# Small parameters of the heads and sinks in one array, and one cache load further back in the load queue

## The chip, the cores and the metric

The kernel runs on one core of one Trainium2 chip. The metric is the device time of one execution in microseconds (us). Before the change it is 1283.69 us, the median of three runs (1283.01 to 1283.9).

TensorE (PE) multiplies, VectorE (DVE), ScalarE (ACT) and GpSimd (POOL) do the elementwise work, and SyncE (SP) issues almost every transfer between HBM and on-chip memory.

## The reference, cut to what matters

One step of an encoder with four layers (A, B, C, A) over 512 prompt tokens and 64 sample tokens of width 1024, all in fp32. Each layer computes

```python
z = rmsnorm(x, norm_g) @ w_in                 # q, k, v and a gate
q = rmsnorm(q_per_head, q_g); k = rmsnorm(k_per_head, k_g)
o = attend(q, k, v, scale, bias, mask, sinks) # sinks in layer B alone
x = x + (o * silu(gate)) @ w_out
```

The small parameters are `q_g` and `k_g` of each layer (128 numbers in A, 64 in B, 96 in C) and B's 16 `sinks`, which enter the softmax of each head as one more score. B also reads a cache of 128 older keys per key head (`cache_bkT`).

## The kernel before, in words

**Precision.** A product is formed from high and low halves: a tile `ws` of weights is split into `wh` (ACT, line 121) and `wl` = `ws` - `wh` (line 122; on POOL in the first microseconds, later on DVE), and the same is done with the transposed activations `T` (ACT line 182 for the high half, DVE line 183 for the low one). Three matmuls (lines 164, 165, 166) then make one product.

**Start.** The five token tiles of `x` (four of 128 rows, one of 64) are loaded, normalised and transposed in `norm`. Each tile takes two halves of 512 columns: DVE scales a half (line 194, output `qs`, or `half` for the tile of 64 rows), PE transposes it with four instructions (`t`, line 179), ACT and DVE write the high and low half of `T`. Between the transposes PE already runs the first matmuls of layer A on the tiles that are there. The weights for these come in four transfers (line 129); the next weights, eight tiles `ws` of two transfers each, come after `flip` and `flip2` (line 132). There are four buffers `ws`, two PSUM buffers `t`, three buffers `qs`. A buffer `ws` is free for the next load when its `wl` has been computed.

**Order.** A scheduler decides at build time the order of the instructions on each engine; each engine then runs its own list in that order and waits where an input is missing. A transfer on SP's list also waits for the one eight places before it on that list (they share one of eight completion counters). That is the program's own rule. It has one effect on reading the profile: a wait for a transfer can be put down to a later transfer on the same counter. The instruction `nsks` (line 467) waits in the program for the two `sks` loads, and the profile names `cqg` for it.

**Small parameters.** Layers A, B and C load them where they are first written in the source (lines 276 and 110, 456 to 465, 688), and the scheduler put most of these loads, and B's cache load (line 482), among the first weight loads of layer A. The sinks per pair of heads are read with a stride:

```python
ld(sks[64 * e : 64 * e + 64], I["b_sinks"].rearrange("o (j e) -> o j e", e=2)[:, :, e].to_broadcast([64, 8]))
```

A few DVE instructions scale or negate them (lines 277, 458, 462, 467, 689), in the order that the scheduler gave them among DVE's other work.

**End of a layer.** `load_x` reads `x` again (line 105), `gain` the next norm's weights (line 936), and `out_proj` loads `w_out` in two halves of eight tiles (line 132), multiplies and adds; `norm` then makes the next `T`.

Of the kernel before, what the change touches and what calls it, by code (L numbers as in the profile page):

```python
# [9 lines left out]
F32 = mybir.dt.float32  # L10
# [4 lines left out]
ALU = mybir.AluOpType  # L15
# [4 lines left out]
KD = 8  # L20
SEQ = 512
DEC = 64
TOK = SEQ + DEC
# [8 lines left out]
CT = (7,)  # L32
# [4 lines left out]
WT = 2 * TOK + DEC  # L37
# [3 lines left out]
def encoder_step(ctx: ExitStack, tc: tile.TileContext, I, O):  # L41
    nc = tc.nc
    V, S, G, PE = nc.vector, nc.scalar, nc.gpsimd, nc.tensor
    ld = nc.sync.dma_start

    const = ctx.enter_context(tc.tile_pool(name="const", bufs=1))
# [7 lines left out]
    def sb(n, tag, bufs=None, dt=F32, pool=work):  # L54
        return pool.tile([128, n], dt, tag=tag, name=tag, bufs=bufs)
# [23 lines left out]
    flip = sb(128, "flip", pool=const)  # L79
    flip2 = sb(128, "flip2", pool=const)  # L80

    mhalf = sb(1, "mhalf", pool=const)
    V.memset(mhalf, -0.5)

# [11 lines left out]
        return half[turn[0]]  # L96

    x = []
    weng = [V]

    def load_x(pool, src):
        x.clear()
        for t, (t0, tn) in enumerate(TT):
            xt = sb(D, f"x{t}", pool=pool)
            ld(xt[:tn], src[t0 : t0 + tn, :])
            x.append(xt)

    def col(src, n, tag, parts=128):
        c = sb(n, tag, pool=const)
        ld(c[:parts], src)  # L110
        return c

    def rstd(ss, tn, n, inv):
        r = sb(n, "nv", pool=tiny)[:tn]
# [70 lines left out]
    def norm(t, g, xT):  # L185
        t0, tn = TT[t]
        ss = sb(1, "nss", pool=tiny)[:tn]
        junk = sb(D, "sq", 2, dt=BF16)[:tn]
        S.activation(junk, x[t][:tn], AF.Square, accum_out=ss)
        r = rstd(ss, tn, 1, 1.0 / D)  # L190
        for hf in range(2):
            xs = rows_of(tn)
            cs = slice(hf * 512, hf * 512 + 512)
            V.scalar_tensor_tensor(out=xs[:tn], in0=x[t][:tn, cs], scalar=r, in1=g[:tn, cs], op0=ALU.mult, op1=ALU.mult)
            pt = v3(ps_t(), 128)
            for j in range(4):
                tr(pt[:, j, :], xs[:, j * 128 : j * 128 + 128])
            k0 = hf * 4
            l0 = lo_at(t0, TOK)
            hl_evac(xT[:, k0 : k0 + 4, t0 : t0 + tn], xT[:, k0 : k0 + 4, l0 : l0 + tn], pt[:, :, :tn])  # L200
            if tn == DEC:
                V.tensor_copy(xT[:, k0 : k0 + 4, 2 * TOK : WT], xT[:, k0 : k0 + 4, TOK : TOK + DEC].bitcast(F32))

    def og_tiles():
        pairs = [v3(sb(2 * TOK, f"o{b}", pool=ogp), TOK) for b in range(KD // 2)]
# [36 lines left out]
    def mix(main, fill):  # L242
        n, f = len(main), 0
        for i, u in enumerate(main):
            u()
            while f < len(fill) * (i + 1) // n:
                fill[f]()
                f += 1
# [23 lines left out]
    def layer_a(li, xT, first=None):  # L272
        w = I["a_w_in"][li]
        with tc.tile_pool(name=f"la{li}", bufs=1, reuse_waits="tile") as lp:
            qg = sb(1, f"qg{li}", pool=const)
            ld(qg, I["a_q_norm"][li].rearrange("(p o) -> p o", o=1))
            V.tensor_scalar(out=qg, in0=qg, scalar1=128 ** -0.5, scalar2=None, op0=ALU.mult)
            kg = col(I["a_k_norm"][li].rearrange("(p o) -> p o", o=1), 1, f"kg{li}")
            ogs, _ = og_tiles()
            vs, qks = {}, {}  # L280

# [167 lines left out]
    def layer_b(xT):  # L449
        w = I["b_w_in"][0]  # L450
        with tc.tile_pool(name="lb", bufs=1, reuse_waits="tile") as lp:
            qg = sb(1, "bqg", pool=const)
            kg = sb(1, "bkg", pool=const)
            for e in range(2):
                r = slice(64 * e, 64 * e + 64)
                ld(qg[r], I["b_q_norm"][0].rearrange("(p o) -> p o", o=1))
                ld(kg[r], I["b_k_norm"][0].rearrange("(p o) -> p o", o=1))
            V.tensor_scalar(out=qg, in0=qg, scalar1=64 ** -0.5, scalar2=None, op0=ALU.mult)
            sk = sb(16, "sk", pool=const)
            ld(sk, I["b_sinks"].to_broadcast([128, 16]))  # L460
            nsk = sb(16, "nsk", pool=const)
            V.tensor_scalar(out=nsk, in0=sk, scalar1=-1.0, scalar2=None, op0=ALU.mult)
            sks = sb(8, "sks", pool=const)
            for e in range(2):
                ld(sks[64 * e : 64 * e + 64], I["b_sinks"].rearrange("o (j e) -> o j e", e=2)[:, :, e].to_broadcast([64, 8]))
            nsks = sb(8, "nsks", pool=const)
            V.tensor_scalar(out=nsks, in0=sks, scalar1=-1.0, scalar2=None, op0=ALU.mult)
            ogs, pairs = og_tiles()

            def rsb(n, tag, bufs=1):  # L470
# [7 lines left out]
            ld(vc, I["cache_b_v"][0, 0].rearrange("t h d -> t (h d)"))  # L478

            kst = v3(sb(512, "hl", 1), 128)  # L480
            for e in range(2):
                ld(kst[64 * e : 64 * e + 64], I["cache_bkT"].rearrange("h p t -> p h t"))
            split(kch[:, :, :128], kcl[:, :, :128], kst)

            def hl(h, l, src, g):
# [4 lines left out]
            for t, (t0, tn) in enumerate(TT):  # L490
                p = mm_tok(xT, TOK, t0, tn, pieces, 512)
# [5 lines left out]
                r = rstd(ss, tn, 4, 1.0 / 64)  # L497
# [177 lines left out]
    def layer_c(xT):  # L675
        w = I["c_w_in"][0]
        with tc.tile_pool(name="lc", bufs=1, reuse_waits="tile") as lp:
            scale = 96 ** -0.5
            early = [sb(512, "ex", 4) for _ in range(3)]
            qag = early[2]  # L680
            ld(qag, I["c_q_a_norm"].to_broadcast([128, 512]))
            kvg = early[0][:, :256]
            ld(kvg, I["c_kv_a_norm"].to_broadcast([128, 256]))
            qgc = sb(1, "cqg", pool=const)
            kgc = sb(1, "ckg", pool=const)
            for g, nm in ((qgc, "c_q_norm"), (kgc, "c_k_norm")):
                V.memset(g[:96], 1.0)
                ld(g[:64], I[nm][0, :64].rearrange("(p o) -> p o", o=1))
            V.scalar_tensor_tensor(out=qgc[:96], in0=qgc[:96], scalar=scale, in1=kgc[:96], op0=ALU.mult, op1=ALU.mult)
            cs = v3(sb(512, "sq", 2)[:, :160], 32)  # L690
            sn_ = v3(sb(512, "sq", 2)[:, :160], 32)
            for tab, nm in ((cs, "rope_cos"), (sn_, "rope_sin")):
# [3 lines left out]
            for nm in ("c_q_norm", "c_k_norm"):  # L696
# [8 lines left out]
                for (sl, rows) in ((slice(0, 4), 128), (slice(4, 5), 64)):  # L705
                    n = sl.stop - sl.start
                    V.tensor_tensor(out=ta[:rows, sl], in0=cs[:rows, sl], in1=bc(gb[:rows].unsqueeze(1), rows, n, 32), op=ALU.mult)
                    for a, b in ((0, 16), (16, 0)):
                        V.tensor_tensor(out=tb[:rows, sl, a : a + 16], in0=sn_[:rows, sl, a : a + 16],
                                        in1=bc(gb[:rows, b : b + 16].unsqueeze(1), rows, n, 16), op=ALU.mult)  # L710
# [25 lines left out]
            for t, (t0, tn) in enumerate(TT):  # L736
                p = mm_tok(xT, TOK, t0, tn, pieces, 512)
# [3 lines left out]
                r = rstd(ss, tn, 1, 1.0 / 512)  # L741
                c = rows_of(tn)
# [8 lines left out]
            for t, (t0, tn) in enumerate(TT):  # L751
                p = mm_tok(xT, TOK, t0, tn, pieces, 288)
# [4 lines left out]
                r = rstd(ss, tn, 2, [(0, 1, 1.0 / 256), (1, 2, 1.0 / 32)])  # L757
                cf = rows_of(tn)[:, :256]
                c = cf[:tn]
# [13 lines left out]
                k0 = 128 * kt  # L773
# [166 lines left out]
    xT = big_xT()  # L940
    first = []
    weng[0] = G
    with tc.tile_pool(name="xp0", bufs=1) as xp:
        for t, (t0, tn) in enumerate(TT):
            xt = sb(D, f"x{t}", pool=xp)
            ld(xt[:tn], I["x"][t0 : t0 + tn, :])
            x.append(xt)
            if t == 0:
                ld(ident, I["ident"])
                nxt_gain = gain(xp, "a", 0)  # L950
            if t < 4:
                src = I["a_w_in"][0][256 * t : 256 * t + 256, 2048:2304].rearrange("(a p) c -> p a c", p=128)
                h, l = load_w([src], 512, 256)
                first += [(h[:, 256 * i : 256 * i + 256], l[:, 256 * i : 256 * i + 256]) for i in range(2)]
            norm(t, nxt_gain, xT)
        ld(flip, I["flip"])
        ld(flip2, I["flip2"])
    dp = ctx.enter_context(tc.tile_pool(name="dp", bufs=1, space=bass.MemoryType.DRAM))
    x_src = I["x"]
    for i, (kind, li) in enumerate(layers):  # L960
        if kind == "a":
            ogs, tail = layer_a(li, xT, first if i == 0 else None)
        elif kind == "b":
            ogs, tail = layer_b(xT)
        else:
            ogs, tail = layer_c(xT)
        x_new = dp.tile([TOK, D], F32, tag=f"xd{i}", name=f"xd{i}") if i < 3 else O["y"]
        nxt = {}

        def after(t, nh):  # L970
            t0, tn = TT[t]
            if i == 3:
                ld(x_new[t0 : t0 + tn, nh * 512 : nh * 512 + 512], x[t][:tn, nh * 512 : nh * 512 + 512])
            elif nh == 1:
                if "xT" not in nxt:
                    nxt["xT"] = big_xT()
                ld(x_new[t0 : t0 + tn], x[t][:tn])
                norm(t, nxt_gain, nxt["xT"])

        with tc.tile_pool(name=f"op{i}", bufs=1, reuse_waits="tile") as op:  # L980
            oT = v3(sb(KD * WT, "oT", dt=F32R, pool=op), WT)

            def put(b):
                split_o(oT, b, ogs[b])

            units = tail(put)
            late = {"a": (6, 7), "b": (6, 7), "c": CT}[kind]
            mix([lambda b=b: put(b) for b in range(KD) if b not in late], units)
            load_x(op, x_src)
            if i < 3:  # L990
                nxt_gain = gain(op, *layers[i + 1])
            out_proj(I[f"{kind}_w_out"][li], oT, after)
        x_src = x_new
        xT = nxt.get("xT")
# [91 lines left out]
```

## Time and profile before

| | |
|---|---|
| median of three runs | 1283.69 us |
| the profiled execution | 1283.49 us |
| its span | 1281.7 us |
| PE busy in the span | 1244.6 us (97%) |
| DVE, ACT, POOL busy | 715.8, 647.7, 383.6 us |
| PE, DVE and ACT in the chain that ended last | 91%, 4%, 2% |

The span runs from the first to the last instruction in the trace; the execution's own time is 1.8 us longer. PE's share of the chain says that what is worth looking at is where PE stands still, and what it waits for there.

### The profile page before, as it was taken

What the parts mean: (1) busy time and instruction counts of PE and PEld (TensorE: products, weight loads), DVE (VectorE), ACT (ScalarE), POOL (GpSimd) and SP (SyncE); (2) the same over time, 40 slices, a digit from 0 to 9 for tenths busy, and PEclk for the clock granted to TensorE, in tenths of its full rate; (3) what the DMA queues carried; (4) which work ended last, traced back from release to release, by engine and by line L of the source; (5) the groups of instructions that cost most, each with busy time, mean ns of one, the idle gap of its engine ahead of it and who ended that gap; (6) DMA issues with size and microseconds to landing.
All of it is one profiled execution on the core that took longest, in us unless ns stands there. A gap on an engine that the chain in (4) does not pass through costs nothing.

```text
span 1281.7 us, 22153 instructions
## 1 busy us (share of the span) xinstructions
PE 1244.6 (97%) x7927; PEld 1092.5 (85%) x7927; DVE 715.8 (56%) x1983; ACT 647.7 (51%) x1645; POOL 383.6 (30%) x492
## 2 busy tenths in 40 slices
PE   4999999999999999999999999999999999999998
PEld 3889898998889899878898787876788898989986
DVE  3365444452568888626567777675164655444432
ACT  4345353552446676624456768686243454435431
POOL 4331212115025542140266454440401212121150
PEclk8999999999999999999999999999999999999999
DMA  5434141523446322244231101112243352414422
GB/s 165 129 93 137 59 137 50 158 91 107 144 126 226 90 65 73 64 137 150 63 109 46 46 26 51 34 50 66 89 148 116 94 158 66 142 49 136 129 81 70
DMA packets 101725, 127.18 MB, mean 99 GB/s; under 512 B 13296, under 2 KB 79760, under 8 KB 101552
## 3 DMA queue, kind: packets, MB, share of 16 engines
q1 hardware_dynamic: 101616, 125.77, 32.0%
q8 instruction: 62, 1.02, 0.3%
q14 instruction: 47, 0.39, 0.1%
HBM read 105.81 MB, written 24.26 MB: 101 GB/s over the span
## 4 chain that ended last, share of the span: by engine, by line
PE 91%; DVE 4%; ACT 2%; DMA 1%; SPq 1%; issue 1%; POOL 0%; ACTq 0%; DVEq 0%; POOLq 0%
PE mm L164 15%; PE mm L166 15%; PE mm L165 15%; PE t L179 8%; PE mm L224 5%; PE mm L225 5%; PE mm L226 5%; PE mm L169 4%; PE mm L170 4%; PE o L386 3%; PE s L880 2%; PE o L890 2%; PE s L378 2%; PE o L611 1%; DMA x<-in_x 1%
## 5 line engine op out<-in xcount | busy, mean ns | idle before, releaser
L117 POOL TENSOR_TENSOR nv<-nv,mhalf 128x4 f32<-128x4 f32 (+7 forms) x147 | 149.9, 1024 | 471.5 <-DVE nv L116 440.1
L164 PE MATMUL mm<-wh,T 128*128 128x256 f32 (+2 forms) x736 | 246.5, 339 | 3.8 <-ACT T L182 2.8
L166 PE MATMUL mm<-wh,T 128*128 128x256 f32 (+2 forms) x736 | 246.6, 337 | 0.0
L165 PE MATMUL mm<-wl,T 128*128 128x256 f32 (+2 forms) x736 | 243.5, 335 | 0.0
L121 ACT ACTIVATE wh<-ws 128x512 fp32r<-128x512 f32 (+2 forms) x288 | 169.4, 614 | 126.3 <-PE mm L169 76.3
L122 DVE TENSOR_TENSOR wl<-ws,wh 128x512 fp32r<-128x512 f32 (+2 forms) x252 | 170.8, 698 | 47.4 <-ACT wh L121 43.8
L224 PE MATMUL mm<-T,wh 128*128 128x288 f32 x512 | 155.5, 304 | 0.1
L164 PEld LDWEIGHTS mm<-wh,T 128*128 128x128 f32 x736 | 140.9, 192 | 15.5 <-ACT T L182 3.4
L225 PE MATMUL mm<-T,wh 128*128 128x288 f32 x512 | 153.4, 300 | 0.0
L226 PE MATMUL mm<-T,wl 128*128 128x288 f32 x512 | 152.9, 299 | 0.0
L166 PEld LDWEIGHTS mm<-wh,T 128*128 128x128 f32 x736 | 141.0, 192 | 12.1 <-DVE T L183 0.2
L165 PEld LDWEIGHTS mm<-wl,T 128*128 128x128 f32 x736 | 140.7, 192 | 11.7
L232 POOL TENSOR_TENSOR o<-o,sq 128x288 f32<-128x288 f32 x52 | 44.0, 847 | 213.9 <-DVE sq L230 142.3
L164 PE MATMUL mm<-wh,oT 128*128 128x512 f32 x256 | 99.8, 399 | 2.5 <-ACT oT L251 1.9
L166 PE MATMUL mm<-wh,oT 128*128 128x512 f32 x256 | 100.3, 399 | 1.3 <-POOL oT L254 1.3
L165 PE MATMUL mm<-wl,oT 128*128 128x512 f32 x256 | 100.9, 397 | 0.0
L224 PEld LDWEIGHTS mm<-T,wh 128*128 128x128 f32 x512 | 96.2, 188 | 3.4 <-issue 1.9
L225 PEld LDWEIGHTS mm<-T,wh 128*128 128x128 f32 x512 | 96.2, 188 | 2.1 <-issue 1.8
L226 PEld LDWEIGHTS mm<-T,wl 128*128 128x128 f32 x512 | 96.2, 188 | 1.1 <-issue 1.1
L263 DVE TENSOR_TENSOR x<-mm,x 128x512 f32<-128x512 f32 x32 | 21.6, 690 | 118.8 <-PE mm L166 113.9
L179 PE MATMUL t<-ident,qs 128*128 128x128 f32 (+1 forms) x376 | 63.7, 282 | 20.3 <-DVE T L183 9.7
L179 PEld LDWEIGHTS t<-ident,qs 128*128 128x128 f32 (+1 forms) x376 | 46.7, 143 | 29.2 <-issue 14.4
(262 smaller groups left out, 2667.9 us busy)
## 6 DMA issues: line engine op xcount, KB each, us to landing
ws<-in_a_w_in SPq DMA_DIRECT2D x64, 256.0 KB, 3.1
ws<-in_a_w_in SPq DMA_DIRECT2D x128, 128.0 KB, 2.5
ws<-in_b_w_in SPq DMA_DIRECT2D x40, 256.0 KB, 3.0
ws<-in_a_w_out SPq DMA_DIRECT2D x32, 256.0 KB, 3.1
xd<-x SPq DMA_DIRECT2D x12, 512.0 KB, 2.7
x<-xd SPq DMA_DIRECT2D x12, 512.0 KB, 6.6
ws<-in_c_w_in SPq DMA_DIRECT2D x24, 256.0 KB, 3.1
out_akT<-kf SPq DMA_DIRECT2D x8, 576.0 KB, 3.5
```

The source lines that it names most:

```text
L117: G.tensor_tensor(out=r, in0=r, in1=bc(mhalf[:tn], tn, n), op=ALU.pow)
L121: S.activation(h, src, AF.Copy)
L122: (eng or G).tensor_tensor(out=l, in0=src, in1=h.bitcast(F32), op=ALU.subtract)
L164: PE.matmul(out, xh, h[:, ws], start=(i == 0), stop=False)
L165: PE.matmul(out, xh, l[:, ws], start=False, stop=False)
L166: PE.matmul(out, xl, h[:, ws], start=False, stop=(i == last))
L169: PE.matmul(out, xs, h[:, ws], start=(i == 0), stop=False)
L170: PE.matmul(out, xs, l[:, ws], start=False, stop=(i == last))
L179: PE.transpose(out, in_, perm or ident)
L224: PE.matmul(p, wh, xT[:, k, cs], start=(k == 0), stop=False)
L225: PE.matmul(p, wh, xT[:, k, ls], start=False, stop=False)
L226: PE.matmul(p, wl, xT[:, k, cs], start=False, stop=(k == KD - 1))
```

## The change

All head gains and the sinks are laid out on the host as one array `par` of 128 rows and 32 columns, with what was repeated over partitions already repeated. One transfer reads it, right after `flip2`. Four DVE instructions compute the scaled and negated copies `der`, behind the last instruction of the first `norm`. The 13 loads of single parameters and their eight DVE instructions (two of them memsets) go. B's cache load (two transfers) may only be issued after the last `x` load of the first layer.

```diff
+    par = sb(32, "par", pool=const)
+    der = sb(32, "der", pool=const)
...
-            qg = sb(1, f"qg{li}", pool=const)
-            ld(qg, I["a_q_norm"][li].rearrange("(p o) -> p o", o=1))
-            V.tensor_scalar(out=qg, in0=qg, scalar1=128 ** -0.5, scalar2=None, op0=ALU.mult)
-            kg = col(I["a_k_norm"][li].rearrange("(p o) -> p o", o=1), 1, f"kg{li}")
+            qg, kg = der[:, li : li + 1], par[:, 4 + li : 5 + li]
...
-            for e in range(2):
-                r = slice(64 * e, 64 * e + 64)
-                ld(qg[r], I["b_q_norm"][0].rearrange("(p o) -> p o", o=1))
-                ld(kg[r], I["b_k_norm"][0].rearrange("(p o) -> p o", o=1))
-            V.tensor_scalar(out=qg, in0=qg, scalar1=64 ** -0.5, scalar2=None, op0=ALU.mult)
-            sk = sb(16, "sk", pool=const)
-            ld(sk, I["b_sinks"].to_broadcast([128, 16]))
-            nsk = sb(16, "nsk", pool=const)
-            V.tensor_scalar(out=nsk, in0=sk, scalar1=-1.0, scalar2=None, op0=ALU.mult)
-            sks = sb(8, "sks", pool=const)
-            for e in range(2):
-                ld(sks[64 * e : 64 * e + 64], I["b_sinks"].rearrange("o (j e) -> o j e", e=2)[:, :, e].to_broadcast([64, 8]))
-            nsks = sb(8, "nsks", pool=const)
-            V.tensor_scalar(out=nsks, in0=sks, scalar1=-1.0, scalar2=None, op0=ALU.mult)
+            qg, kg = der[:, 2:3], par[:, 6:7]
+            sk, sks, nsk, nsks = par[:, 8:24], par[:, 24:32], der[:, 8:24], der[:, 24:32]
...
-            for e in range(2):
-                ld(kst[64 * e : 64 * e + 64], I["cache_bkT"].rearrange("h p t -> p h t"))
+            with tc.issue_after(late[0]):
+                for e in range(2):
+                    ld(kst[64 * e : 64 * e + 64], I["cache_bkT"].rearrange("h p t -> p h t"))
...
-                ld(g[:64], I[nm][0, :64].rearrange("(p o) -> p o", o=1))
-            V.scalar_tensor_tensor(out=qgc[:96], in0=qgc[:96], scalar=scale, in1=kgc[:96], op0=ALU.mult, op1=ALU.mult)
+            qgc = der[:, 3:4]
...
         ld(flip2, I["flip2"])
+        ld(par, I["par"])
+        with tc.issue_after(end):
+            for a, b, f in ((0, 2, 128 ** -0.5), (2, 3, 64 ** -0.5), (8, 32, -1.0)):
+                V.tensor_scalar(out=der[:, a:b], in0=par[:, a:b], scalar1=f, scalar2=None, op0=ALU.mult)
+            V.scalar_tensor_tensor(out=der[:, 3:4], in0=par[:, 3:4], scalar=96 ** -0.5, in1=par[:, 7:8], op0=ALU.mult, op1=ALU.mult)
...
-            load_x(op, x_src)
+            late[0] = load_x(op, x_src)
```

SP's list behind `flip2` stood like this before the change (`ws` are the weights; the two `hl` are B's cache load):

```order
L957 DMA flip_78<-in_flip 128x128
L276 DMA qg_256<-in_a_q_norm 128x1
L110 DMA kg_259<-in_a_k_norm 128x1
L132 DMA ws<-in_a_w_in 128x256 x2
L456 DMA bqg<-in_b_q_norm 64x1
L457 DMA bkg<-in_b_k_norm 64x1
L456 DMA bqg<-in_b_q_norm 64x1
L132 DMA ws<-in_a_w_in 128x256 x2
L457 DMA bkg<-in_b_k_norm 64x1
L460 DMA sk<-in_b_sinks 128x16
L132 DMA ws<-in_a_w_in 128x256 x2
L465 DMA sks<-in_b_sinks 64x8x1 x2
L132 DMA ws<-in_a_w_in 128x256 x2
L482 DMA hl<-in_cache_bkT 64x4x128 x2
```

The same place of the list now:

```order
L935 DMA flip_78<-in_flip 128x128
L936 DMA par<-in_par 128x32
L131 DMA ws<-in_a_w_in 128x256 x12
L364 DMA bias<-in_a_rel 128x512
L296 DMA out_av<-v 128x256 x2
L131 DMA ws<-in_a_w_in 128x256 x4
```

Twelve weight transfers now stand together behind one small load, where eight stood among nine small loads, with the two cache loads behind them.

DVE's list around the transposes of token tiles 1 to 3 stood like this before (`T` is the low half of the transposed activations, `qs` and `half` the scaled rows, `nsk` and `nsks` the negated sinks):

```order
L277 TENSOR_SCALAR qg_256<-qg_256 128x1
L194 SCALAR_TENSOR_TENSOR qs<-x_190,nv,gain 128x512
L458 TENSOR_SCALAR bqg<-bqg 128x1
L116 TENSOR_SCALAR nv<-nss 64x1
L462 TENSOR_SCALAR nsk<-sk 128x16
L183 TENSOR_TENSOR T<-t,T 128x4x128
L194 SCALAR_TENSOR_TENSOR qs<-x_190,nv,gain 128x512
L467 TENSOR_SCALAR nsks<-sks 128x8
L183 TENSOR_TENSOR T<-t,T 128x4x128
L194 SCALAR_TENSOR_TENSOR half_82<-x_222,nv,gain 64x512
```

And now:

```order
L193 SCALAR_TENSOR_TENSOR qs<-x_192,nv,gain 128x512
L115 TENSOR_SCALAR nv<-nss 64x1
L182 TENSOR_TENSOR T<-t,T 128x4x128
L193 SCALAR_TENSOR_TENSOR qs<-x_192,nv,gain 128x512
L182 TENSOR_TENSOR T<-t,T 128x4x128
L193 SCALAR_TENSOR_TENSOR half_84<-x_224,nv,gain 64x512
L193 SCALAR_TENSOR_TENSOR half_83<-x_224,nv,gain 64x512
```

The four small instructions that stood between them are gone from this place; the rest keeps its order.

At the end of the first layer SP's list now reads:

```order
L108 DMA x_3341<-in_x 64x1024
L914 DMA gain<-in_b_norm 128x1024
L466 DMA hl<-in_cache_bkT 64x4x128 x2
L131 DMA ws<-in_a_w_out 128x512 x8
```

The two cache loads stand there between `gain` and the second half of `w_out`, which followed each other directly before. ACT's and POOL's lists are unchanged, PE's but for two matmuls that moved behind some transposes early in the kernel.

## Rows read from the trace of the kernel before

**Rows 1.** First line of the page.

```profile
span 1281.7 us, 22153 instructions
```

**Rows 2.** Busy time by stretch; last three columns: granted PE clock, DMA share, GB/s.

```profile
24.00:28.00 4.00, 1.75 (x10) 1.46 (x9) 0.00 (x0) 0.00 (x0) 1.15 (x1) 0.54 0.05 0
28.00:34.00 6.00, 0.00 (x0) 0.00 (x0) 0.61 (x2) 0.00 (x0) 0.00 (x0) 0.50 0.40 113
34.30:360.00 325.70, 325.70 (x2023) 292.48 (x2024) 159.40 (x378) 145.24 (x329) 73.50 (x90) 0.99 0.37 113
```

**Rows 3.** Who waited for whom, 0 to 50 us: total, times, longest.

```profile
ACT wh L121 <- DMA ws<-in_a_w_in: 16.4, 4, 10.6
...
DVE nsks L467 <- DMA cqg<-in_c_q_norm: 9.5, 1, 9.5
PE t L179 <- DVE T L183: 9.7, 2, 8.5
...
DVE nsk L462 <- DMA sk<-in_b_sinks: 2.9, 1, 2.9
```

**Rows 4.** Timeline of PE: start, duration, instruction, idle time before it and releaser.

```profile
21.72 0.39 PE L164 MATMUL mm<-wh,T 128*128 128x256 f32 x1 [1.15 <-ACT T L182]
...
23.35 0.63 PE L179 MATMUL t<-ident,qs 128*128 128x128 f32 x4 [1.12 <-DVE T L183]
...
34.30 1.09 PE L179 MATMUL t<-ident,qs 128*128 128x128 f32 x4 [8.55 <-DVE T L183]
...
37.74 0.71 PE L179 MATMUL t<-ident,qs 128*128 128x128 f32 x4
...
39.73 0.60 PE L179 MATMUL t<-ident,half 128*128 128x128 f32 x4
...
41.60 0.60 PE L179 MATMUL t<-ident,half 128*128 128x128 f32 x4
```

**Rows 5.** Timeline of DVE.

```profile
17.05 1.28 DVE L194 SCALAR_TENSOR_TENSOR qs<-x,nv,gain 128x512 f32<-128x512 f32 x1
...
18.33 0.73 DVE L194 SCALAR_TENSOR_TENSOR qs<-x,nv,gain 128x512 f32<-128x512 f32 x1
...
22.43 0.18 DVE L462 TENSOR_SCALAR nsk<-sk 128x16 f32<-128x16 f32 x1 [2.93 <-DMA sk<-in_b_sinks]
22.52 0.68 DVE L183 TENSOR_TENSOR T<-t,T 128x512 fp32r<-128x512 f32 x1
...
33.39 0.17 DVE L467 TENSOR_SCALAR nsks<-sks 128x8 f32<-128x8 f32 x1 [9.53 <-DMA cqg<-in_c_q_norm]
```

**Rows 6.** Timeline of ACT.

```profile
17.53 0.57 ACT L182 ACTIVATE T<-t 128x512 fp32r<-128x512 f32 x1
...
20.56 0.63 ACT L121 ACTIVATE wh<-ws 128x512 fp32r<-128x512 f32 x1 [1.93 <-DMA ws<-in_a_w_in]
...
34.36 0.63 ACT L121 ACTIVATE wh<-ws 128x512 fp32r<-128x512 f32 x1 [10.57 <-DMA ws<-in_a_w_in]
```

**Rows 7.** Timeline of POOL.

```profile
16.50 1.29 POOL L122 TENSOR_TENSOR wl<-ws,wh 128x512 fp32r<-128x512 f32 x1 [0.23 <-ACT wh L121]
```

**Rows 8.** Timeline of SP's issues at the start.

```profile
17.62 1.00 SPq L132 DMA_DIRECT2D ws<-in_a_w_in  x2
...
20.76 1.33 SPq L465 DMA_DIRECT2D sks<-in_b_sinks  x2
```

**Rows 9.** Issues from 0 to 50 us: count, KB each, median us to landing.

```profile
ws<-in_a_w_in SPq DMA_DIRECT2D x21, 128.0 KB, 2.7
...
hl<-in_cache_bkT SPq DMA_DIRECT2D x2, 128.0 KB, 11.2
```

**Rows 10.** The tile `sks`: time from issue to landing of its two loads.

```profile
DMA to landing us min/median/max: 8.6/10.2/11.8
```

**Rows 11.** Timeline of SP's issues at the first layer's end.

```profile
291.87 0.33 SPq L936 DMA_DIRECT2D gain<-in_b_norm  x1
298.03 26.91 SPq L132 DMA_DIRECT2D ws<-in_a_w_out  x8
```

More of the change, by code (lines that the diff above doesn't have):

```diff
@@ L98, in encoder_step @@
     x = []
+    late = [None]
     weng = [V]
@@ L104, in load_x @@
             xt = sb(D, f"x{t}", pool=pool)
-            ld(xt[:tn], src[t0 : t0 + tn, :])
+            last = ld(xt[:tn], src[t0 : t0 + tn, :])
             x.append(xt)
[L108 to L111, printed above, removed]
+        return last.ins
     def rstd(ss, tn, n, inv):
@@ L201, in norm @@
             if tn == DEC:
-                V.tensor_copy(xT[:, k0 : k0 + 4, 2 * TOK : WT], xT[:, k0 : k0 + 4, TOK : TOK + DEC].bitcast(F32))
+                end = V.tensor_copy(xT[:, k0 : k0 + 4, 2 * TOK : WT], xT[:, k0 : k0 + 4, TOK : TOK + DEC].bitcast(F32))
+        return end.ins if tn == DEC else None
     def og_tiles():
@@ L451, in layer_b @@
         with tc.tile_pool(name="lb", bufs=1, reuse_waits="tile") as lp:
-            qg = sb(1, "bqg", pool=const)
-            kg = sb(1, "bkg", pool=const)
-            for e in range(2):
-                r = slice(64 * e, 64 * e + 64)
-                ld(qg[r], I["b_q_norm"][0].rearrange("(p o) -> p o", o=1))
-                ld(kg[r], I["b_k_norm"][0].rearrange("(p o) -> p o", o=1))
-            V.tensor_scalar(out=qg, in0=qg, scalar1=64 ** -0.5, scalar2=None, op0=ALU.mult)
-            sk = sb(16, "sk", pool=const)
-            ld(sk, I["b_sinks"].to_broadcast([128, 16]))
-            nsk = sb(16, "nsk", pool=const)
-            V.tensor_scalar(out=nsk, in0=sk, scalar1=-1.0, scalar2=None, op0=ALU.mult)
-            sks = sb(8, "sks", pool=const)
-            for e in range(2):
-                ld(sks[64 * e : 64 * e + 64], I["b_sinks"].rearrange("o (j e) -> o j e", e=2)[:, :, e].to_broadcast([64, 8]))
-            nsks = sb(8, "nsks", pool=const)
-            V.tensor_scalar(out=nsks, in0=sks, scalar1=-1.0, scalar2=None, op0=ALU.mult)
+            qg, kg = der[:, 2:3], par[:, 6:7]
+            sk, sks, nsk, nsks = par[:, 8:24], par[:, 24:32], der[:, 8:24], der[:, 24:32]
             ogs, pairs = og_tiles()
@@ L677, in layer_c @@
         with tc.tile_pool(name="lc", bufs=1, reuse_waits="tile") as lp:
-            scale = 96 ** -0.5
             early = [sb(512, "ex", 4) for _ in range(3)]
@@ L683, in layer_c @@
             ld(kvg, I["c_kv_a_norm"].to_broadcast([128, 256]))
[L684 to L687, printed above, removed]
-                ld(g[:64], I[nm][0, :64].rearrange("(p o) -> p o", o=1))
-            V.scalar_tensor_tensor(out=qgc[:96], in0=qgc[:96], scalar=scale, in1=kgc[:96], op0=ALU.mult, op1=ALU.mult)
+            qgc = der[:, 3:4]
             cs = v3(sb(512, "sq", 2)[:, :160], 32)
@@ L954, in encoder_step @@
                 first += [(h[:, 256 * i : 256 * i + 256], l[:, 256 * i : 256 * i + 256]) for i in range(2)]
-            norm(t, nxt_gain, xT)
+            end = norm(t, nxt_gain, xT)
         ld(flip, I["flip"])
         ld(flip2, I["flip2"])
+        ld(par, I["par"])
[3 more added lines that the diff above has]
+            V.scalar_tensor_tensor(out=der[:, 3:4], in0=par[:, 3:4], scalar=96 ** -0.5, in1=par[:, 7:8], op0=ALU.mult, op1=ALU.mult)
     dp = ctx.enter_context(tc.tile_pool(name="dp", bufs=1, space=bass.MemoryType.DRAM))
@@ L986, in encoder_step @@
             units = tail(put)
-            late = {"a": (6, 7), "b": (6, 7), "c": CT}[kind]
-            mix([lambda b=b: put(b) for b in range(KD) if b not in late], units)
-            load_x(op, x_src)
+            after_gate = {"a": (6, 7), "b": (6, 7), "c": CT}[kind]
+            mix([lambda b=b: put(b) for b in range(KD) if b not in after_gate], units)
+            late[0] = load_x(op, x_src)
             if i < 3:
@@ L1043 @@
     arrays["x"] = np.concatenate([a["x_prompt"][0], a["x_sample"][0]], 0)
-    for nm in ("a_w_in", "a_q_norm", "a_k_norm", "a_w_out", "b_w_in", "b_q_norm", "b_k_norm", "b_sinks", "b_w_out",
+    for nm in ("a_w_in", "a_w_out", "b_w_in", "b_w_out",
                "c_w_in", "c_q_a_norm", "c_w_qb", "c_kv_a_norm", "c_w_kvb", "c_q_norm", "c_k_norm", "c_w_out",
@@ L1052 @@
     arrays["cache_ckvT"] = a["cache_c_kv"][0, 0].T
+    wide = lambda v: np.tile(v, 128 // v.shape[0])
+    rest = lambda v: np.concatenate([v[:64], np.ones(64, np.float32)])
+    cols = [a["a_q_norm"][0], a["a_q_norm"][1], wide(a["b_q_norm"][0]), rest(a["c_q_norm"][0]),
+            a["a_k_norm"][0], a["a_k_norm"][1], wide(a["b_k_norm"][0]), rest(a["c_k_norm"][0])]
+    sinks = a["b_sinks"][0]
+    arrays["par"] = np.concatenate([np.stack(cols, 1), np.tile(sinks, (128, 1)),
+                                    np.repeat(sinks.reshape(8, 2).T, 64, axis=0)], 1).astype(np.float32)
     arrays = {f"in_{k}": np.ascontiguousarray(v) for k, v in arrays.items()}
```

## The prediction

> **What bounds the kernel now.** I read the kernel from the whole to the stage. The span is 1281.7 us [rows 1]; the profiled execution took 1283.49 us, so 1.8 us lie outside the span, and the median of the runs, 1283.69, is 0.2 us from it. The busy times by stretch come next [rows 2]: from 34.3 to 360 us PE is busy 325.70 of 325.70 us. There is no gap in which a late transfer or a late DVE instruction could show, so whatever moves the start of that stretch moves everything behind it by as much. Ahead of it PE has 1.75 us of work between 24 and 28 us and none between 28 and 34, and the transfers do next to nothing in the first of these stretches (share 0.05, 0 GB/s). This is not bandwidth; something small is holding the queue.
>
> The waits of the first 50 us say what [rows 3]. PE's longest wait is 8.5 us for DVE's low half of `T`. DVE's longest is 9.5 us, in front of `nsks`, ACT's 10.6 us for a weight tile. In the program `nsks` waits for the two `sks` loads; the profile's `cqg` is a later user of the same counter. The timelines join the pieces: the `sks` loads are issued from 20.76 us on [rows 8] and need 8.6 and 11.8 us to land [rows 10] although they move 2 KB each, and the cache loads issued behind them need 11.2 us, where a weight transfer of the same 128 KB needs 2.7 at the median [rows 9]. So DVE stands at `nsks` until 33.39 [rows 5], ACT at the fourth weight tile until 34.36 [rows 6], and PE resumes at 34.30 after 8.55 us [rows 4].
>
> Two shorter gaps lie ahead of it, with the same cause in small. At 23.35 PE has waited 1.12 us for a low half of `T` [rows 4] which DVE started at 22.52 only because it had stood 2.93 us at `nsk`, waiting for `sk` [rows 5]; its input, ACT's high half, was there at 17.53 + 0.57 = 18.1 [rows 6]. At 21.72 PE has waited 1.15 us for ACT [rows 4], which had stood 1.93 us for a weight tile, converted at 20.56 [rows 6]; that tile's two transfers were issued at 17.62 [rows 8], behind five small loads.
>
> **What the change takes out.** I follow one instruction, the transposes of the second half of token tile 3, at 37.74 before [rows 4]. Everything from there on has the same order on PE.
>
> - The wait at `nsks`, and the late fourth weight tile with it: 8.55 us of PE.
> - The wait at `nsk`: 1.12 us.
> - The late second weight tile: 1.15 us. Together 10.82 us.
> - The clock. The granted clock was 0.54 of full from 24 to 28 us and 0.50 from 28 to 34 [rows 2], that is the level of 1.2 GHz after PE had stood twice for over a microsecond and then altogether; before those gaps and after 38 us it is the level of 2.4 GHz. One half of a token tile (four transposes and twelve matmuls) takes 41.60 - 39.73 = 1.87 us at full clock, and 37.74 - 34.30 = 3.44 at the lower: 1.57 lost. The half after that took 39.73 - 37.74 = 1.99: 0.12 lost. The stretch from 23.35 to the start of the long gap (34.30 - 8.55 = 25.75) took 2.40; it holds a half less the two matmuls that already ran at 21.72 (two twelfths of some 1.4 us of matmuls, 0.24), 1.63 at full clock: 0.77 lost. Together 2.46. If PE no longer stops there, nothing lets the clock fall.
>
> Gross this is 13.3 us: the instruction would move from 37.74 to 24.4.
>
> **What is late next.** For that, ACT must have the fourth weight tile and DVE the low half of `T` for the half before it.
>
> The weight tile: its buffer is free when POOL ends at 16.50 + 1.29 = 17.79 [rows 7]; two issues take 1.00 [rows 8], landing takes 2.7 [rows 9], so it is there at some 21.5 and its conversion and the high half of `T` behind it (0.63 and 0.57) [rows 6] are done at 22.7. PE needs them at 24.2. That holds with 1.5 us to spare.
>
> DVE: from 19.1 (18.33 + 0.73) it has to do, in its list's order, a low half of `T`, a `qs`, a low half, two `half`, and the low half in question, that is 3 x 0.68 + 3 x 0.73 = 4.2 us [rows 5], so it ends at 23.3, 1.1 us before PE wants it. But this holds only if POOL is quiet. A `qs` took 0.73 us at 18.33, and 1.28 at 17.05 [rows 5], where POOL was computing `wl` from 16.50 to 17.79 [rows 7]: it ended 0.54 us after POOL did. Before, POOL stood idle from 25 to 35 us with everybody else; now three `wl` of 1.29 us each stand back to back just where DVE has these three instructions. If each takes 1.28, DVE ends at 25.0 and PE waits 0.6 us; if each waits for a whole `wl` (1.29 more), at 27.2, and PE waits 2.8; with none, nothing. I take 0.6, as the one stretched row is the nearest, and keep 0 and 2.8 for the range. The Trainium skill gives the reason (GPSIMD Engine Reference, section 1, Specifications): GpSimd shares its SBUF interfaces with VectorE and contends with DVE instructions that have two SBUF inputs. The two rows agree with it; by that rule at its hardest, POOL always first, the gain would be 10.5 us.
>
> Left over: 13.3 - 0.6 = 12.7 us.
>
> **What the change adds.** The load `par` (128 rows of 128 bytes) takes the place of one of the removed loads on SP. The trace has no row of its form; `sk` (64 bytes a row, 2.93 us of waiting [rows 5]) lies below it and `sks` (8.6 and 11.8 us [rows 10]) above it in cost. It is contiguous in each row like `sk`, so I take some 3 us, up to 7 while the first weights still hold the queue. Even 11.8 us would end at about 22, when the only thing that waits for it is the issue of a weight transfer eight places on; that would cost up to 3 us of ACT's 1.5 to spare, so 1.5 at worst. The four `der` instructions run after the last `norm` instruction on DVE, in a stretch where DVE has nothing that PE waits for (before, two of the removed instructions ran at that place, and PE had no gap); 0 us.
>
> The cache loads move behind `gain`. SP issues `gain` at 291.87 and then nothing until 298.03 [rows 11]. The two issues fit into these 5.8 us, even at 2 us each, and their data is wanted in layer B, some 60 us on. 0 us; if the eight `w_out` loads behind them were held, each microsecond beyond 5.8 would be one lost at most. The removed second set for the last layer, the `c` parameters and their DVE instructions all lay beside a busy PE: 0 us.
>
> The Trainium skill's advice here is another sum (DMA: Bandwidth & Descriptors, Anatomy of one DMA and Rules for kernel authors): each transfer has about 2.0 us of fixed cost, so small ones should be coalesced; twelve transfers fewer would by that give 24 us, an estimate from that page, if they ran one after another. The trace speaks against adding them up: SP issues one in some 0.5 us with several under way, and PE stood still for 10.82 us in all.
>
> **The rivals.** (a) *More is given back*: DVE or the weight tiles are late by so much that PE stops again for over a microsecond and the clock falls. The next two halves at 3.44 instead of 1.87 cost 3.1 us, with a wait of 1 to 2.8: gain 7 to 9, time 1274.5 to 1276.5; with the wait alone, 1272 to 1273. For it: POOL's back-to-back `wl`. Against: DVE had 1.1 us to spare.
> (b) *More is gained*: no clash, and the first weights of the second product come earlier too: 13.3 to 14.5, time 1269.0 to 1270.2.
> (c) *The change doesn't do it*: the slow queue is not the strided `sks` but the start of the kernel itself, and the weight tile is as late as before behind other transfers. Then DVE is free but ACT waits to 34.36, and PE with it: 1283 to 1284. Against: the first `sks` load took 8.6 us [rows 10] though it was issued before the cache loads, in the middle of weights of which the median landed in 2.7.
> (d) *Slower*: the cache loads at 292 us hold SP's list, for instance because they land as slowly as before (11.2 us each) and `w_out` waits for them. To be slower than before it must cost more than 12.7 us, that is hold SP for more than 5.8 + 12.7 = 18.5 us; one landing is 11.2, both in a row 22.4, which would give 1283.5 - 12.7 + 16.6 = 1287. Against: the waits that could hit them lie eight places on, when 20 us have passed.
>
> **How the numbers follow.** The likeliest case is 1283.5 - 12.7 = 1270.8 us (0.60, own range 1269.7 to 1272.0). (a) has 0.20, (b) 0.12, (c) 0.05, (d) 0.03. The range from 1268.8 to 1274.5 holds the likeliest case, (b) and the milder half of (a). The runs before lie within 0.9 us of each other, so 0.2% (2.6 us) is about what can be told from no change: faster has 0.92, the same 0.05, slower 0.03.
>
> **What would show it.** In the changed kernel's trace: DVE has no wait for a parameter; ACT has no wait of over 2 us for weights between 18 and 30 us; PE has no idle microsecond between 14 and 60 us; the granted clock of 20 to 40 us is near 1.00; the first transposes of `half` come at about 27 us instead of 39.73; every later stretch is the same, shifted by 12.7 us; the cache loads at about 280 us change no gap. I would be wrong if PE stops anew at the low half of `T` with POOL busy, if the fourth weight tile still lands after 25 us, or if PE's busy stretch has new gaps later.

## The result, and the profile after

The changed kernel takes 1273.15 us (median of four runs, 1272.26 to 1273.75), the kernel before 1283.8 in the same measurement (1283.01 to 1284.04). The ratio is 0.9918 with a 95% interval of 0.99 to 0.9935: faster by 10.6 us, where 12.7 were forecast. The profiled execution took 1273.74 us; its span is the first row of its page:

```profile
span 1272.0 us, 22132 instructions
```

The busy times by stretch answer to [rows 2]:

```profile
24.00:28.00 4.00, 1.09 (x10) 0.89 (x8) 3.98 (x3) 0.53 (x2) 2.67 (x4) 1.00 0.43 118
28.00:34.00 6.00, 5.97 (x38) 5.97 (x39) 2.10 (x4) 1.54 (x4) 0.20 (x2) 0.72 0.66 188
34.30:350.00 315.70, 315.70 (x1961) 282.83 (x1960) 153.62 (x370) 140.18 (x319) 70.62 (x86) 1.00 0.36 110
```

The stretch from 28 to 34 us, which was empty, is full. But PE still has only 1.09 us of work between 24 and 28, and DVE, which did nothing there before, is now busy for 3.98 us with three instructions. The granted clock falls to 0.72 behind that gap, that is a mix of the two levels, 2.4 and 1.2 GHz. From 34.3 us PE is busy throughout, as before.

The waits of the first 50 us answer to [rows 3]:

```profile
ACT v L294 <- DVE half L193: 4.6, 1, 4.6
...
PE t L178 <- DVE T L182: 2.9, 1, 2.9
ACT wh L120 <- DMA ws<-in_a_w_in: 2.9, 1, 2.9
```

No DVE instruction waits for a parameter any more, and ACT's only wait for weights stands before 18 us. What is left is one wait of PE for DVE's low half of `T`, 2.9 us instead of 8.5 [rows 3]. PE's timeline shows the place; it answers to [rows 4]:

```profile
21.19 0.60 PE L178 MATMUL t<-ident,qs 128*128 128x128 f32 x4
...
23.06 0.60 PE L178 MATMUL t<-ident,qs 128*128 128x128 f32 x4
...
28.03 0.66 PE L178 MATMUL t<-ident,qs 128*128 128x128 f32 x4 [2.94 <-DVE T L182]
...
31.04 1.05 PE L178 MATMUL t<-ident,half 128*128 128x128 f32 x4
...
33.37 0.60 PE L178 MATMUL t<-ident,half 128*128 128x128 f32 x4
```

The instruction that the prediction follows stands at 28.03; it was to be at 24.4 gross and 25.0 with the give-back. Take the wait away and it is at 25.09. DVE's and POOL's timelines say what DVE did meanwhile (DVE's answers to [rows 5]):

```profile
17.62 2.35 DVE L193 SCALAR_TENSOR_TENSOR qs<-x,nv,gain 128x512 f32<-128x512 f32 x2
...
19.96 0.67 DVE L182 TENSOR_TENSOR T<-t,T 128x512 fp32r<-128x512 f32 x1
...
22.56 4.82 DVE L193 SCALAR_TENSOR_TENSOR half<-x,nv,gain 64x512 f32<-64x512 f32 x2
27.30 0.67 DVE L182 TENSOR_TENSOR T<-t,T 128x512 fp32r<-128x512 f32 x1
```

```profile
20.19 1.30 POOL L121 TENSOR_TENSOR wl<-ws,wh 128x512 fp32r<-128x512 f32 x1 [1.42 <-ACT wh L120]
...
22.41 3.75 POOL L121 TENSOR_TENSOR wl<-ws,wh 128x512 fp32r<-128x512 f32 x3
```

Two `half` took 4.82 us. The view of the tile `half` gives shortest, median and longest of DVE's eight in the whole kernel, in ns:

```profile
L193 DVE SCALAR_TENSOR_TENSOR half<-x,nv,gain x8: 733/740/4156, 22.6 to 954.2; 64x512 f32<-64x512 f32 x8
```

So the first took 4.16 us and the second about 0.7. It began at 22.56, 0.15 us after POOL's three `wl`, and ended at 26.72, 0.56 us after the last of them (22.41 + 3.75 = 26.16). In this kernel it did not get in between two `wl`; it stood until POOL's row had ended.

Two rows more close the list of [rows 10, 11]. The parameter load, in the view of `par`, and SP's issues at the first layer's end:

```profile
L936 SPq DMA_DIRECT2D par<-in_par x1: 328/328/328, 10.4 to 10.4; - x1
...
DMA to landing us min/median/max: 8.1/8.1/8.1
```

```profile
283.64 0.33 SPq L914 DMA_DIRECT2D gain<-in_b_norm  x1
284.02 1.31 SPq L466 DMA_DIRECT2D hl<-in_cache_bkT  x2
289.80 26.91 SPq L131 DMA_DIRECT2D ws<-in_a_w_out  x8
```

`par` took 8.1 us to land, and nothing waited for it. The two cache loads fill 1.31 us of SP's idle time: from `gain` to `w_out` it is 289.80 - 283.64 = 6.16 us, before 298.03 - 291.87 = 6.16 [rows 11].

### The profile page after: what moved, and what is told of

It reads as the page before. It is cut to its first block, busy times and chain, and to the rows that moved or that the text cites. A ratio compares the mean times of both kernels' runs of the same rounds, so it can differ in the third digit from the quotient of the medians.

```text
span 1272.0 us, 22132 instructions
## 1 busy us (share of the span) xinstructions
PE 1242.3 (98%) x7927; PEld 1090.7 (86%) x7927; DVE 719.3 (57%) x1979; ACT 647.7 (51%) x1645; POOL 383.1 (30%) x492
## 4 chain that ended last, share of the span: by engine, by line
PE 94%; DVE 2%; ACT 2%; DMA 1%; issue 0%; POOL 0%; SPq 0%; DVEq 0%; POOLq 0%; ACTq 0%
PE mm L163 16%; PE mm L165 16%; PE mm L164 16%; PE t L178 9%; PE mm L224 5%; PE mm L225 5%; PE mm L226 5%; PE mm L168 4%; PE mm L169 4%; PE o L383 3%; PE s L858 3%; PE o L868 2%; PE s L375 2%; PE o L595 1%; PE s L562 1%; PE s L563 1%
```

## The experiments

The seven kernels ran in two groups. The median of before was 1283.18 us beside the changed kernel again, all four `wl` behind the `half`, the parameters alone and the stride alone; it was 1283.99 beside the other three.

**The changed kernel again**, unedited, beside the runs that follow.

> The changed kernel as it is, beside the others on the same chip. All theories: 1272 to 1274 us, PE waits about 2.9 us once for DVE's low half of T near 28 us, and the granted clock falls to half for some microseconds behind it.

It took 1272.88 us (1270.62 to 1275.72), ratio 0.9922 [0.9909, 0.9934]. In its profile the longest `half` is 4170 ns and PE's wait for the low half of `T` 2.2 us, and the granted clock from 28 to 34 us is 0.74. The stall belongs to the kernel, not to one execution.

**POOL's `wl` behind the `half`.** The four `wl` of the next product are issued behind the first memset of `v`, which itself waits for DVE's two `half`. Order on the other engines stays.

```diff
+        with tc.issue_after(hold[0]):      # hold: the first memset of v, layer 0 only
+            (eng or G).tensor_tensor(out=l, in0=src, in1=h.bitcast(F32), op=ALU.subtract)
```

> The changed kernel with POOL's wl of the next product's first four weight tiles put behind the memset of v, which waits for DVE's two half instructions. Theory (POOL's back-to-back wl hold off DVE's two-input half instructions): each half takes about 0.7 us instead of 2.4, PE's wait of 2.9 us near 28 us goes, the clock stays at full, and the time falls by 4 to 4.8 us to about 1268.6. Rival (DVE is late for another reason, such as its own list or ACT's high half): the halves stay long or PE waits elsewhere for as long, 1272 to 1274. Second rival (the later wl become what PE waits for): PE waits for POOL's wl near 33 us, above 1274.

It took 1267.59 us (1267.25 to 1268.16), ratio 0.9881 [0.9866, 0.9896], 5.3 us faster than the changed kernel beside it, where 4 to 4.8 were expected. The timelines of DVE, POOL and PE, and the busy time from 20 to 40 us:

```profile
19.57 1.40 DVE L198 SCALAR_TENSOR_TENSOR half<-x,nv,gain 64x512 f32<-64x512 f32 x2
...
23.43 0.69 DVE L187 TENSOR_TENSOR T<-t,T 128x512 fp32r<-128x512 f32 x1 [1.18 <-ACT T L186]
```

```profile
21.47 5.04 POOL L126 TENSOR_TENSOR wl<-ws,wh 128x512 fp32r<-128x512 f32 x4
```

```profile
24.04 0.60 PE L183 MATMUL t<-ident,qs 128*128 128x128 f32 x4
...
25.91 0.60 PE L183 MATMUL t<-ident,half 128*128 128x128 f32 x4
```

```profile
20.00:40.00 20.00, 20.00 (x136) 18.48 (x136) 5.77 (x15) 7.27 (x14) 10.91 (x12) 1.00 0.61 191
```

With POOL out of the way the `half` take 0.70 us each, PE has no gap from 20 to 40 us, and the clock stays at its upper level. The followed instruction is at 24.04, 37.74 - 24.04 = 13.7 us ahead of before [rows 4], where the prediction's gross sum had 13.3. POOL's work is not lost, only moved to where DVE has no instruction with two SBUF inputs.

**One `wl` left beside the `half`.** As above, but only the last two of the four are held.

```diff
-        if hold[0] is None:
+        skip[0] -= 1                       # 2 at the start of the held product
+        if hold[0] is None or skip[0] >= 0:
```

> The changed kernel with only the last two of POOL's four wl for the next product issued behind DVE's two half; one wl is left beside them. Theory (each half, with two SBUF inputs, stands while POOL runs a wl): the two half take 2.6 to 3.2 us instead of 4.8 (one stretched, one 0.70), PE's wait for the low half of T falls from 2.2 to 2.9 us to at most 1, the clock doesn't fall, and the time is 1267.5 to 1270. Rival (the half are slow for another reason, such as the weight transfers landing meanwhile): they still take 4.8 us, and the time stays at 1272 to 1274.

It took 1268.34 us (1267.93 to 1270.48), ratio 0.9881 [0.9868, 0.9895]. The two `half` take 2.34 us, a little less than expected, and PE's wait is 0.28:

```profile
21.33 2.34 DVE L200 SCALAR_TENSOR_TENSOR half<-x,nv,gain 64x512 f32<-64x512 f32 x2
23.59 0.67 DVE L189 TENSOR_TENSOR T<-t,T 128x512 fp32r<-128x512 f32 x1
```

```profile
24.33 0.66 PE L185 MATMUL t<-ident,qs 128*128 128x128 f32 x4 [0.28 <-DVE T L189]
```

One `wl` beside them costs about 1 us (2.34 - 1.40), three cost 3.4 (4.82 - 1.40): in these runs the price goes by the `wl` that stand in a row. DVE's spare time swallows nearly all of the first; it is the second and third that stop PE. Weight transfers are not what slows the `half`: 165 GB/s moved from 19.5 to 21 us in the run above, where the `half` take 0.70 each, and 115 GB/s from 22.5 to 26.7 us in the changed kernel, where the first takes 4.16.

**The parameters alone.** The changed kernel with the cache loads left free, as before.

```diff
-            with tc.issue_after(late[0]):
-                for e in range(2):
-                    ld(kst[64 * e : 64 * e + 64], ...)
+            for e in range(2):
+                ld(kst[64 * e : 64 * e + 64], ...)
```

> The changed kernel with B's cache load left free, so that the scheduler puts it among the first weight loads again. Theory (the strided sinks loads alone held the queue): the two cache loads land in under 5 us each, the weights behind them are late by 1 us or less, 1272 to 1275. Rival (the cache loads were part of what held the queue): weights land later by 3 us or more and PE stops for ACT, 1277 or more.

It took 1272.45 us (1272.34 to 1273.03), ratio 0.9918 [0.9905, 0.9932], with the same wait of 3.0 us at PE. All of the gain is the parameters'. The cache loads landed in 5.6 us at the median, a little over the 5 that were expected.

**The cache loads alone.** The kernel before with only these two loads moved; one DVE instruction on layer C's gains is tied to its old place.

```diff
+            with tc.issue_after(late_x[0]):
                 for e in range(2):
                     ld(kst[64 * e : 64 * e + 64], ...)
```

> The kernel before, with only layer B's two cache loads moved behind the first layer's residual loads; the two strided sinks loads and the other ten small loads stay where they were. Theory (the 4-byte stride of the sinks loads holds the queue): the two loads still take 8 to 12 us to land, DVE stands some 9 us at nsks and PE some 8.5 us behind it, and the time is that of the kernel before, 1282 to 1284 us. Rival (the 256 KB of cache loads in the queue right behind the sinks loads make everything there late): DVE's wait at nsks falls below 4 us, PE's below 3, and the time to 1274 to 1278.

It took 1283.45 us (1282.61 to 1285.09), ratio 0.9999 [0.999, 1.0009]. Its waits and its `sks` landings are nearly those of before [rows 3, 10] (the profile names `qg`, a later load on the same counter, for the `sks` loads):

```profile
PE t L182 <- DVE T L186: 9.4, 2, 7.9
...
DVE nsks L472 <- DMA qg<-in_a_q_norm: 8.8, 1, 8.8
```

```profile
DMA to landing us min/median/max: 8.3/9.9/11.4
```

So the 256 KB behind the sinks loads were victims of the slow queue, not its cause.

**The stride alone.** The kernel before with the two strided sinks loads replaced by one contiguous load of the same 128 x 8 numbers; all other small loads stay.

```diff
-            for e in range(2):
-                ld(sks[64 * e : 64 * e + 64], I["b_sinks"].rearrange("o (j e) -> o j e", e=2)[:, :, e].to_broadcast([64, 8]))
+            ld(sks, I["sks"])
```

> The kernel before with one edit that matters: the two strided sks loads are one load of an array laid out as 128 rows of 8 numbers (the last instruction on the c parameters is held at its old place on DVE). All other small loads stay. Theory (the stride is the cause): the load lands in under 4 us, DVE does not wait 9.5 us at nsks, the fourth weight tile is not late by 10 us, and the time falls by 6 to 10 us, to 1274 to 1278, with the wait at nsk left. Rival (the number of small loads is the cause, each with its own fixed cost): one of fifteen loads is gone, the gain is under 2 us, 1282 or more.

It took 1273.61 us (1271.42 to 1275.99), ratio 0.9927 [0.9915, 0.994]. Two DVE rows, three PE rows and the view of `sks`:

```profile
22.45 0.17 DVE L465 TENSOR_SCALAR nsk<-sk 128x16 f32<-128x16 f32 x1 [2.96 <-DMA sk<-in_b_sinks]
...
23.80 0.16 DVE L469 TENSOR_SCALAR nsks<-sks 128x8 f32<-128x8 f32 x1
```

```profile
21.63 0.39 PE L165 MATMUL mm<-wh,T 128*128 128x256 f32 x1 [1.01 <-ACT T L183]
...
23.37 0.63 PE L180 MATMUL t<-ident,qs 128*128 128x128 f32 x4 [1.24 <-DVE T L184]
...
28.45 0.60 PE L180 MATMUL t<-ident,qs 128*128 128x128 f32 x4
```

```profile
DMA to landing us min/median/max: 2.5/2.5/2.5
```

The same numbers at the same place land in 2.5 us instead of 8.6 and 11.8 [rows 10], and DVE no longer waits at `nsks`. The wait at `nsk` stays, 2.96 us. This one edit brings 9.6 us (1283.18 - 1273.61), within the 6 to 10 expected and nearly all that the whole change brought. That does not make the eleven other small loads free. PE's two short gaps (1.01 and 1.24 us) stay, the granted clock from 24 to 28 us is 0.57, and the followed instruction stands at 28.45, 4.4 us behind the run with all four `wl` behind the `half` (24.04), which has none of these loads; 0.56 of the 4.4 is that run's earlier start. The two totals come out alike because the changed kernel loses about as much at its `half`, while here the two `half` together take 1.88 us and PE does not wait for them.

**The strided loads, with nobody waiting.** The changed kernel plus the two strided loads at the front of SP's list, into a tile that nothing reads.

```diff
+            for e in range(2):
+                ld(idle[64 * e : 64 * e + 64], I["b_sinks"].rearrange("o (j e) -> o j e", e=2)[:, :, e].to_broadcast([64, 8]))
```

> The changed kernel plus the two strided sinks loads of before, at the front of SP's list (one behind the parameter load, one a weight tile later) into a tile that nobody reads; all else stays. Theory (a strided load holds up the transfers behind it on the queue, whoever reads it): the weight transfers behind them land 5 to 10 us late, ACT waits 3 to 9 us for a weight tile, PE stops behind ACT and the clock falls, 1276 to 1283 us. Rival (what cost time was only DVE standing at nsks for its own load): no instruction waits for these loads, and the time stays at 1272 to 1274.

It took 1276.4 us (1276.18 to 1276.75), ratio 0.9941 [0.9928, 0.9953]: 3.5 us over the changed kernel by the medians (1276.4 - 1272.88), 2.4 by the ratios to before (0.9941 and 0.9922), at the lower edge of what the theory gave, with a gap of 2.9 us at PE and ACT's wait of 5. ACT's row, PE's row, and the count of packets from 0 to 50 us:

```profile
25.79 0.63 ACT L120 ACTIVATE wh<-ws 128x512 fp32r<-128x512 f32 x1 [4.96 <-DMA ws<-in_a_w_in]
```

```profile
26.96 0.58 PE L163 MATMUL mm<-wh,T 128*128 128x256 f32 x1 [2.90 <-ACT T L181]
```

```profile
DMA packets 8625, 9.12 MB, mean 182 GB/s; under 512 B 1968, under 2 KB 7664, under 8 KB 8624
```

The changed kernel has 912 packets under 512 B in that time, this one 1968. The 1056 more are about one for each of the 2 x 64 x 8 = 1024 numbers. The Trainium skill has that rule (DMA: Bandwidth & Descriptors, Rules for kernel authors): a strided last dimension is lowered to one descriptor (the order for one run of bytes) per element. The packet counts agree. The rival, that only DVE's own wait cost time, falls: nothing reads these loads, and ACT still waits 4.96 us for the weights behind them. The 2.4 to 3.5 us are not a clean price, though. PE's gap stands in the place of the changed kernel's own 2.94, and in this profile SP was already late at the last `x` load (8.71 us, in the changed kernel 6.22), ahead of both strided loads (12.63 and 16.78).

DVE and POOL meet otherwise here. These are the two `half` and POOL's three `wl` in a row:

```profile
27.55 2.46 DVE L193 SCALAR_TENSOR_TENSOR half<-x,nv,gain 64x512 f32<-64x512 f32 x2
```

```profile
26.50 4.66 POOL L121 TENSOR_TENSOR wl<-ws,wh 128x512 fp32r<-128x512 f32 x3 [3.33 <-ACT wh L120]
```

One by one the `half` took 0.77 and 1.75 us, the second and third `wl` 1.72 and 1.74. The engines took turns, and POOL's row took 0.91 us longer than in the changed kernel (4.66 - 3.75). What decides between taking turns and standing for the whole row was not tested.

## Why the prediction was right, point by point

The time fell inside the range and on the forecast side, but the likeliest case's own range (1269.7 to 1272.0) missed it: what happened at PE is rival (a).

- *The waits removed.* Right: no wait at `nsk`, at `nsks` or for the late weight tiles. That the strided `sks` were the cause is shown from both sides, taken out of before (1273.61) and put back into the change (1276.4, with ACT's wait of 4.96 us for weights). The two short gaps belong to the other small loads: they are still there with contiguous sinks, and gone with the parameters in one array. Rival (c) is out.
- *The gross sum, 13.3 us with the clock.* Right: 13.7 where nothing is given back (`wl` behind the `half`; 0.56 of it is that profile's earlier start, token tile 1's transposes at 13.03 and before at 13.59), 13.4 with one `wl` left (37.74 - 24.33).
- *The give-back, 0.6 us: the term that was mis-sized.* It measured 2.94 us. The prediction named the place, the engines and the bound (2.8, "POOL always first"), and then chose the value from the one stretched `qs` row, which stood beside a single `wl` [rows 5, 7]. It charged each DVE instruction a delay of its own; in the changed kernel the first `half` stood for the whole row of `wl` (4.16 us, 4.17 in the repeat, 4.24 with the parameters alone) and the second ran free, but with the idle strided loads the engines took turns, so this is no rule. The Trainium skill states the kind of contention (SBUF — State Buffer, SBUF: two separate sides): the pair of ports that VectorE and GpSimd share is an exclusive lock, held for a whole instruction, against a DVE instruction with two SBUF inputs. The `half` beside one `wl` agrees (1.68 us in the run with one `wl` left, 0.73 alone), and so does the low half of `T` at 23.43 in the run with all four behind the `half`: one of its inputs is in PSUM, and it took 0.69 us in the middle of the four `wl`. That a waiting `half` lets three `wl` by is measured here. By its bound the prediction had a gain of 10.5; 10.6 was measured, though partly by luck, as the next points show.
- *The clock.* It was to stay up; it fell behind that wait, as rival (a) has it. The prediction's own first sign of being wrong, a new stop of PE at the low half of `T` with POOL busy, came true. From the followed instruction to the second `half` transposes PE took 33.37 - 28.03 = 5.34 us, before 41.60 - 37.74 = 3.86 [rows 4]: 1.48 lost. There the profile stands at 41.60 - 33.37 = 8.23 us of gain, inside the 7 to 9 of rival (a), and not at the 12.7 forecast.
- *The start.* The first 20 us hold some 0.4 us more than before in this profile (transposes of token tile 1 at 14.00 and 13.59). This slip was not there in the repeated run, so no part of the change is charged with it.
- *What came back.* The profile's gain is 1281.7 - 1272.0 = 9.7 us, 1.5 more than the 8.23 at 42 us. Nearly all of that is one place in layer B, the last section.
- *`par` at some 3 us.* Mis-sized: 8.1, within the bound of 11.8; the cover that the prediction named (eight issues before anyone waits) held. *`der`, the removed second set, the cache loads at 0 us:* right, and the cache loads alone measured 0.9999. Rival (d) is out.
- *The sum of 24 us by a fixed cost for each transfer.* Rightly set aside: 10.6 us were measured. The section of the Trainium skill that the prediction drew on (DMA: Bandwidth & Descriptors, Anatomy of one DMA) gives the 2.0 us for transfers that GpSimd issues. SP issues these, and no run here shows the figure.

A version with the change and POOL's `wl` held back beats both kernels, at 1267.59 us.

## What to carry to other kernels

Find the one small transfer that is slow before counting how many there are: here the two read with a stride, one number at a time, cost nearly ten microseconds by themselves. The eleven others cost PE two gaps of about a microsecond each and some of its clock, which the totals hid behind the new stall. When a stall goes, everything that used to be spread out by it comes together; ask which two engines now work at the same time on the same ports, and allow for the waiting one to stand for the whole row of the other's instructions, not for one. A second engine's work that nobody needs yet is best placed behind the instruction that it would block.

## What was not expected of the hardware

The first is that 4.16 us `half`: three separate `wl` in a row, and DVE's instruction, already begun, got in after none of them, while with the idle strided loads a `half` got in after each of the first two. The other is the clock in layer B. Before two gaps of 1.0 and 1.3 us that both kernels have, PE was busy at the upper level; behind them the kernel before ran at 0.57 for a while and the changed one did not. Here is before, then after, at the same instructions:

```profile
540.00:546.00 6.00, 4.23 (x30) 3.25 (x28) 2.35 (x4) 5.59 (x13) 3.43 (x4) 1.00 0.60 168
546.00:550.00 4.00, 3.43 (x8) 2.76 (x9) 0.45 (x1) 1.71 (x4) 4.00 (x7) 0.57 0.98 383
```

```profile
532.00:538.00 6.00, 4.08 (x28) 3.15 (x28) 2.35 (x4) 5.74 (x13) 3.58 (x4) 1.00 0.58 174
538.00:542.00 4.00, 3.57 (x15) 2.73 (x16) 0.46 (x1) 1.57 (x4) 4.00 (x7) 1.00 1.03 389
```

PE issues eight matmuls there in the one and fifteen in the other. It is worth 1.4 us: matched instructions are 8.15 us apart ahead of it (540.04 and 531.89) and 9.53 behind it (551.00 and 541.47). The clock also fell there in the profiles of the cache loads alone and of the contiguous sinks (0.71 from 533 to 541 us), and in none of the other five runs. Whether a kernel meets it or an execution does was not settled: one profile of each kernel can't tell, and nothing in the change touches this place. Executions of one kernel do differ: those of the contiguous sinks go from 1271.42 us at a mean granted clock of 0.999 to 1275.99 at 0.995.
